# A decoder layer on one core: where the squares of x, the storing of weight parts and the V joins stand in a hand-written order

## The chip, the core and the metric

The kernel runs on one core of one Trainium2 chip. The metric is the device time of one execution in microseconds (us), as the median of the runs. The engines named below are TensorE (PE for its matmuls, PEld for its weight loads), VectorE (DVE), ScalarE (ACT), GpSimd (POOL, here mostly an issuer of transfers) and SyncE (SP, which issues most transfers).

## The reference

One layer of a decoder for 1024 positions of width 2048, all in float32. The input is normalised, and one projection makes the queries, keys, values and gates of two groups of eight heads: a stick-breaking group ("sb" below) and a differential group ("df", two softmax maps subtracted). Both outputs are gated, joined, projected and added to the residual; then a per-layer embedding is gated with a sigmoid of the normalised residual and added, and a last norm closes.

```python
hn = rmsnorm(h, norm_mix_g[i])
proj = hn @ w_in[i]
sb_q, sb_k, sb_v, sb_g, df_q, df_k, df_v, df_g = jnp.split(proj, split_at, axis=-1)
sb_out = stick_breaking_attention(sb_q, sb_k, sb_v)        # (1, 1024, 8, 128)
df_out = differential_attention(dq, dk, df_v, lam)         # rotary on a quarter of each q and k
df_out = rmsnorm(df_out, subln_g[i], SUBLN_EPS) * (1.0 - lambda_init)
mixed = jnp.concatenate([sb_out * jax.nn.silu(sb_g), df_out * jax.nn.silu(df_g)], axis=-1)
h = h + mixed @ w_out[i]
gate = jax.nn.sigmoid(rmsnorm(h, norm_ple_g[i]) @ w_ple_gate[i])
h = h + gate * (p[i] @ w_ple_proj[i])
return rmsnorm(h, norm_final_g)
```

## The kernel before

Every float32 product is made of three matmuls of split operands (high by high, high by low, low by high), so every weight tile is cast once to its high part (on ACT) and subtracted once for its low part (on DVE) before PE can use it. The 1024 rows are two halves of 512; the causal maps are made for half 1 first, then for half 0.

The stages, by time in the profile: up to about 630 us the V and gate columns of the projection; 630 to 1080 us the q and k products and the attention of half 1; 1080 to 1640 us the same for half 0; then the output projection (to about 1960 us) and the embedding's gate (to the end).

**The first stage** is an instance `gv` of the class `Seven`. It makes each pair of output blocks out of seven products instead of eight (a Strassen-like scheme with summed inputs S1 to S4 and summed weights T, L761), for 16 units of columns. One product is twelve matmuls of 512 columns, some 2.72 us, and is called a slot: `Seven.step` is run after each, casts the next weight tiles (`wpr`, L802 on ACT and L816 on DVE), does what is due and calls `chore(slot)`. In the first phase a unit has five slots (S2, A22, S1, S4, S3, where A22 and S4 are of the unit before), in the second phase, from slot 79 on, seven (A11, A22, S2, S4, A12, S1, S3). What follows a product is also fixed: for S3 the sum `u` on DVE (L1242 in the kernel before), after which the PSUM bank `pbc` can be written by the next unit.

**What hangs on the slots** besides the products, in `chore`:

- The sum of squares of x for the norm (`square`): 32 tiles `xs` of 128x512 are loaded by SP (L1057); three slots later ACT squares one (L1061 for the first of each half, L1063) and DVE adds it to `ssa` (L1064). `TICK["rows"]` is the slot of the first. The tiles have the tag "xt", four buffers that they share with the `xv` tiles of the sums S1 to S4 just ahead of them (stored to `xcomb_d` by POOL), with the chores' tiles and, later, with the V joins.
- `joint`: the sums over the partitions and the Newton steps of the square root, at fixed slots.
- The chores themselves: 32 weight tiles (of `w_out` and of the last pair of heads' `w_in`) that will be needed later as parts are loaded (`craw`, L1122), split into `chi` (ACT L1127) and `clo` (DVE L1128), and stored by SP (L1117, L1118).

**The attention** runs over pairs of heads, a df head and then an sb head, while PE makes the q and k products of the next (`acc`, L295 to L297). What stands beside them on DVE and ACT is placed in a queue of steps by ticks (`Side.add`, `side.later`; 32 ticks to a unit of products). The table `TICK` holds all ticks; a name with `mid_` or `end_` ahead replaces the plain one for the last pair of half 1 and of half 0 (`tk`). The steps that matter here, for a row block of a df head: scores `z` on PE (L381 to L388), row maximum on DVE (L435, `mx`), exponential on ACT (L443, `et`), the inverse of the sums and lambda on DVE (L448, L449), a scaling on ACT (L453), the difference of the two maps on DVE (L458, `et`), its transposes on PE (L493, `tp`), their split in two parts (L511 and L512 on ACT, L516 `lead` and L517 `awl` on DVE), and the product with V on PE (L535 to L540, `av`). `values` joins V for one head: it comes from DRAM as two planes of 16-bit halves (`vf`), is put together by two ACT copies (L474, `vw`), cast to its high part on ACT (L475) and subtracted on DVE (L478). In half 1 it is also stored for half 0.

For PE, DVE and ACT the program's order is the order written by hand (`tc.manual_schedule`); SP and POOL are ordered by the scheduler. In the middle seam ("turn"), where half 1 hands over to half 0, ACT and DVE also make the split x of half 0 (`xh` L1315, `xl` L1316).

Of the kernel before, what the change touches and what calls it, by code (L numbers as in the profile page):

```python
# [39 lines left out]
GLAT = {'S4': 4, 'S1': 4, 'S2': 4, 'S3': 3}  # L40
TICK = {
    "neg": 2, "cs": 27, "x0_at": (7, 7, 8, 7), "end_df_soft": (1, 1.5, 4.5, 5.5), "df_inv": 4, "mid_df_inv": 2.7,
    "end_df_inv": 4.5, "sumlag": 2, "gvx": ((22, 27), (80, 85)), "chore": (85, 0, 0), "rows": 19, "opx": (8, 12), "turn": 76, "lag":
    15, "gap": (4, 6), "parts": (1, 2), "vparts": (2, 3), "sums": (0, 2), "squared": (3, 4.5), "norm": (1, 4), "df_scores":
    (-20, -16, -13, -8, -4, 0, 4, 8), "df_turn": (19, 19), "df_v": -6, "df_norm": 44.5, "sb_scores": (-2, 5.5, 13.5, 22),
    "sb_turn": (32, 36), "sb_v": 19, "df_soft": (1, 1.5, 4, 5.5), "sb_stick": (1, 1, 3, 5.5), "taken": (28, 31), "sb_split":
    (1, 2), "kv": 9, "df_vg": (25, 42, 58, 59.5), "sb_vg": (4, 16, 24, 25.5), "q_turn": (-1.0, 5.5, 5, 6.5, 10, 12,
# [5 lines left out]
    70), "begun": (86.5, 91.5, 93.5, 94.5, 93.5), "mid_turn": 76, "mid_lag": 17, "mid_gap": (4, 7), "mid_df_scores": (-20,  # L53
    -16, -9, -8.5, -1, -0.5, 4, 8), "mid_df_turn": (19, 17), "mid_df_v": -6, "mid_df_norm": 44.5, "mid_sb_scores": (-3, 5,
    12.5, 21), "mid_sb_turn": (32, 36), "mid_sb_v": 18, "mid_taken": (28, 31), "mid_q_turn": (-1.5, 4.5, 4.5, 5.5, 9.5,
    11.5, 12.5), "mid_k_turn": (-1.5, 8, 8.5, 9, 13.5, 15, 16, 17.5), "end_turn": 76, "end_lag": 15, "end_gap": (4, 6),
    "end_df_scores": (-23, -16, -15, -8, -4, 0, 4, 8), "end_df_turn": (18.5, 19), "end_df_v": -6, "end_df_norm": 44.5,
    "end_sb_scores": (-2, 6, 13.5, 22), "end_sb_turn": (32, 36), "end_sb_v": 19, "end_taken": (28, 31), "end_q_turn": (-1.0,
    5, 5, 6.5, 10, 12, 13.5), "end_k_turn": (-4.5, 8, 8.5, 10, 13.5, 15, 16, 17.5),
}  # L60
# [4 lines left out]
def build(nc, tc, ap):  # L65
    with ExitStack() as ctx:
        _body(ctx, nc, tc, ap)


def _body(ctx, nc, tc, ap):  # L70
# [7 lines left out]
    V, G, A, T = nc.vector, nc.gpsimd, nc.scalar, nc.tensor  # L78
# [200 lines left out]
    side = Side()  # L279
# [67 lines left out]
    def attention(at, pz, half, hd, q, qz, K, KL, VV, sg, vg, rcol):  # L347
# [119 lines left out]
        def values():  # L467

            v = at.tile([P, 2, 4, P], F32R, name="v", tag="v")
            whole = ev.tile([P, 4, P], F32, name="vw", tag="xt", bufs=4)  # L470
            words = whole.bitcast(U16).rearrange("p a (b c) -> p a b c", c=2)
            planes = vg[0].bitcast(U16).rearrange("p (c a b) -> p c a b", c=2, a=4)
            for c in range(2):
                A.copy(words[:, :, :, c], planes[:, c])  # L474
            side.later(TICK["vparts"][0], lambda: A.copy(v[:, 0], whole))  # L475

            def low():
                V.tensor_tensor(v[:, 1], whole, v[:, 0].bitcast(F32), op=ALU.subtract)  # L478
                if half == 1:
                    G.dma_start(v_d[hd], v.rearrange("p a b c -> p (a b c)"))  # L480

            side.later(TICK["vparts"][1], low)
            VV.insert(0, v)

        def turn(pr, g):
# [147 lines left out]
    with tc.tile_pool(name="at", bufs=2) as at, tc.tile_pool(name="pz", bufs=2, space=PSUM) as pz:  # L633
# [420 lines left out]
        def square(kt, hf):  # L1054

            t = ev.tile([P, HALF], F32, name="xs", tag="xt", bufs=4)
            nc.sync.dma_start(t, xsrc(hf, kt))  # L1057

            def fn():
                if kt == 0:  # L1060
                    A.activation(ssa[hf], t, AF.Square)  # L1061
# [33 lines left out]
        chores = deque()  # L1095
# [5 lines left out]
        work, done = [], []  # L1101

        rows = deque((kt, hf) for kt in range(NK) for hf in (1, 0))
        fetched = deque()

        def chore(slot):
            q = slot - TICK["rows"]
            if q >= 0 and fetched and fetched[0][0] <= slot:
                fetched.popleft()[1]()
            if q >= 0 and rows and (q * 11) % 16 < 11:  # L1110
                fetched.append((slot + 3, square(*rows.popleft())))
            if slot in joint:
                joint.pop(slot)()
            if slot % 3 == 0 and done:
                (hi, lo), hi_d, lo_d = done.pop()
                if hi_d is not None:
                    nc.sync.dma_start(hi_d.bitcast(F32), hi.bitcast(F32))  # L1117
                nc.sync.dma_start(lo_d.bitcast(F32), lo.bitcast(F32))  # L1118
            if slot % 3 == 0 and chores and slot >= TICK["chore"][0] and not TICK["chore"][1] <= slot < TICK["chore"][2]:
                src, hi_d, lo_d = chores.popleft()  # L1120
                raw = ev.tile([P, HALF], F32, name="craw", tag="xt", bufs=4)
                nc.sync.dma_start(raw, src)  # L1122
                work.append((raw, hi_d, lo_d))
            elif slot % 3 == 2 and work:
                raw, hi_d, lo_d = work.pop()
                hi, lo = [ev.tile([P, HALF], F32R, name=nm, tag="xt", bufs=4) for nm in ("chi", "clo")]
                A.copy(hi, raw)  # L1127
                V.tensor_tensor(lo, raw, hi.bitcast(F32), op=ALU.subtract)  # L1128
                done.append(((hi, lo), hi_d, lo_d))
# [32 lines left out]
        def root(hf):  # L1162
            A.activation(ssa[hf], totals[hf], AF.Ln, bias=eps6[:, 0:1], scale=1.0 / NK)
            A.activation(ssa[hf], ssa[hf], AF.Exp, scale=-0.5)
            rstds[hf] = ssa[hf]

        def refined(hf, i):
            if i == 0:
                steps[hf] = ev.tile([P, HALF], F32, name="nt", tag="xt", bufs=4)
            t, ps, r = steps[hf], totals[hf], ssa[hf]  # L1170
            if i == 0:
                V.scalar_tensor_tensor(t, ps, EPS * NK, r, op0=ALU.add, op1=ALU.mult)
            elif i == 1:
                V.scalar_tensor_tensor(t, t, -0.5 / NK, r, op0=ALU.mult, op1=ALU.mult)
            else:
                V.scalar_tensor_tensor(r, t, 1.5, r, op0=ALU.add, op1=ALU.mult)

        joint = {67: partial(split_sum, 1), 68: partial(split_sum, 0), 70: lambda: (total(1), total(0)), 71: partial(root, 1), 73: partial(root, 0)}
        joint.update({72 + i: partial(refined, 1, i) for i in (0, 2)})
        joint[73] = lambda: (refined(1, 1), root(0))  # L1180
        joint.update({75 + i: partial(refined, 0, i) for i in range(3)})
        joint[79] = consts_late

        parts_of = {}

# [291 lines left out]
        for half in (1, 0):  # L1477
            X = X0 if half == 0 else X1

            for hd in ORDER:  # L1480
# [110 lines left out]
                q, k, qz, KL = qk[0], qk[1], qk.get("qz"), qk.get("kl")  # L1591
# [894 lines left out]
```

## Time and profile before

| | |
|---|---|
| median of 3 runs | 2323.59 us (2322.37 to 2324.1) |
| the profiled execution | 2324.44 us, of which 2322.6 us are the profile's span |
| granted TensorE clock, mean | 0.998 |
| PE matmuls | 2294.8 us busy, 99% of the span |
| DVE | 1816.6 us, 78% |
| ACT | 1341.1 us, 58% |
| POOL | 320.9 us, 14% |
| transfers | 565.05 MB, 243 GB/s on average |

A line of the timeline has the start in us, the duration, the engine, the line of the program, the operation and what it writes from what it reads; brackets at its end hold the idle time of that engine just before, and what ended it. A group of several instructions in one line has their count behind an x. A line of waits has the engine and the operation that waited, what for, and then the total, the number and the longest in us. A line of windows has the stretch and its length, then busy us of PE, PEld, DVE, ACT and POOL with their counts, the granted clock, the share of the DMA engines' time and GB/s. Because the matmuls' ends are modelled and overlap, a stall of PE is seen earlier in the weight load's record (PEld) than in the matmul's.

### The profile page before, as it was taken

The page shows a single profiled execution, that of the slowest core. Times are in us where ns is not written, and L with a number is a line of the kernel's source. Part 1 is how long each engine was busy: PE and PEld are TensorE (multiplying, and loading weights), DVE is VectorE, ACT ScalarE, POOL GpSimd, SP SyncE. Part 2 cuts the span into 40 slices and gives each one's busy share as a digit, 9 for nine tenths or more (in the row PEclk, how much of TensorE's full clock was granted, in tenths as well). Part 3 has the DMA queues.
Part 4 walks back from the last instruction along what each step waited for, and adds up shares of the span by engine and source line. Part 5 has one row for each costly group of instructions (what it writes and reads, how often), then busy time and mean ns, then how long its engine had stood idle before and what let it go on. Part 6 is the DMA issues. An engine that isn't in the chain of part 4 may idle for free.

```text
span 2322.6 us, 32653 instructions
## 1 busy us (share of the span) xinstructions
PE 2294.8 (99%) x10961; PEld 1916.6 (83%) x10961; DVE 1816.6 (78%) x3155; ACT 1341.1 (58%) x2420; POOL 320.9 (14%) x498
## 2 busy tenths in 40 slices
PE   9999999999999999999999999999999999999998
PEld 7877888888788888887888888888888888888887
DVE  6578887777668888878778777778787988687787
ACT  6424354444357777778877777777733435542555
POOL 2121111111211111101011001110121121111000
PEclk9999999999999999999999999999999999999999
DMA  8687678877798888899676677777999789998975
GB/s 260 214 295 252 202 247 239 247 211 199 208 271 276 244 256 240 250 282 315 199 218 186 182 208 209 204 199 239 269 213 244 248 246 282 313 357 269 298 239 199
DMA packets 290200, 565.05 MB, mean 243 GB/s; under 512 B 62688, under 2 KB 73184, under 8 KB 290032
## 3 DMA queue, kind: packets, MB, share of 16 engines
q1 hardware_dynamic: 219216, 383.34, 53.0%
q0 software_dynamic: 58864, 158.10, 24.7%
q10 hardware_dynamic: 11952, 21.53, 2.6%
q8 instruction: 86, 1.41, 0.3%
q14 instruction: 82, 0.67, 0.1%
HBM read 359.16 MB, written 203.69 MB: 242 GB/s over the span
## 4 chain that ended last, share of the span: by engine, by line
PE 61%; issue 18%; DVE 8%; DMA 4%; ACT 4%; POOL 3%; SPq 0%; POOLq 0%; DVEq 0%; ACTq 0%
PE acc L297 8%; PE acc L295 8%; PE acc L296 8%; PE pbc L707 7%; PE pa L707 5%; PE pc L707 4%; PE tp L493 2%; POOL vg_d L915 2%; PE pb L707 2%; PE av L540 1%; PE av L539 1%; PE av L538 1%; PE pc L1904 1%; PE pc L1903 1%; PE pc L1902 1%
## 5 line engine op out<-in xcount | busy, mean ns | idle before, releaser
L802 ACT CAST wpr<-T 128x512 fp32r<-128x512 f32 x208 | 127.3, 620 | 423.1 <-DVE T L761 362.8
L295 PE MATMUL acc<-xh,whi 128*128 128x512 f32 x768 | 310.2, 404 | 0.0
L297 PE MATMUL acc<-xh,wlo 128*128 128x512 f32 x768 | 300.6, 391 | 0.0
L296 PE MATMUL acc<-xl,whi 128*128 128x512 f32 x768 | 300.5, 391 | 0.0
L297 PEld LDWEIGHTS acc<-xh,wlo 128*128 128x128 f32 x768 | 144.2, 188 | 31.8
L295 PEld LDWEIGHTS acc<-xh,whi 128*128 128x128 f32 x768 | 145.1, 189 | 25.1
L296 PEld LDWEIGHTS acc<-xl,whi 128*128 128x128 f32 x768 | 144.8, 189 | 24.4
L802 ACT CAST wpr<-wraw 128x512 fp32r<-128x512 f32 x128 | 78.6, 617 | 124.5 <-DMA wraw<-tw_d 37.3
L816 DVE TENSOR_TENSOR wpr<-T,wpr 128x512 fp32r<-128x512 f32 x208 | 142.4, 685 | 8.4 <-ACT wpr L802 6.7
L200 ACT CAST whi<-wraw 128x1024 fp32r<-128x1024 f32 x128 | 134.3, 1049 | 13.4 <-DMA wraw<-w_in 7.4
L443 ACT ACTIVATE et<-z,mx 128x512 f32<-128x512 f32 (+7 forms) x128 | 94.8, 741 | 56.9 <-DVE mx L435 56.5
L707 PE MATMUL pbc<-cA,wpr 128*128 128x512 f32 x480 | 117.5, 394 | 5.0 <-DVE u L1242 4.6
L517 DVE TENSOR_TENSOR awl<-tp,awh 128x256 fp32r<-128x256 f32 (+1 forms) x160 | 92.6, 579 | 33.5 <-ACT awh L512 32.9
L707 PE MATMUL pc<-cS,wpr 128*128 128x512 f32 x480 | 115.3, 389 | 0.0
L707 PE MATMUL pbc<-cS,wpr 128*128 128x512 f32 x480 | 115.3, 389 | 0.0
L707 PEld LDWEIGHTS pbc<-cA,wpr 128*128 128x128 f32 x480 | 90.3, 189 | 26.6 <-DVE u L1242 7.5
L435 DVE CUSTOM_DVE_ANT_0 z<-z,wide 128x512 f32<-128x512 f32 (+7 forms) x128 | 97.5, 763 | 18.5 <-PE z L388 16.0
L707 PE MATMUL pbc<-cS2h,wpr 128*128 128x512 f32 x320 | 105.7, 391 | 0.0
L707 PEld LDWEIGHTS pc<-cS,wpr 128*128 128x128 f32 x480 | 90.1, 188 | 18.7
L707 PEld LDWEIGHTS pbc<-cS,wpr 128*128 128x128 f32 x480 | 90.1, 188 | 18.7
L707 PE MATMUL pc<-cS4h,wpr 128*128 128x512 f32 x320 | 105.0, 389 | 0.0
L915 POOL DMA_DIRECT2D vg_d<-hc x96 | 62.6, 652 | 302.1 <-DVE hc L1140 167.1
(556 smaller groups left out, 6460.4 us busy)
## 6 DMA issues: line engine op xcount, KB each, us to landing
wraw<-w_in SPq DMA_DIRECT2D x128, 512.0 KB, 4.7
wraw<-w_vg SPq DMA_DIRECT2D x143, 256.0 KB, 3.7
wlo_d<-wlo POOLq DMA_DIRECT2D x56, 512.0 KB, 6.5
vg_d<-hc POOLq DMA_DIRECT2D x96, 256.0 KB, 4.3
wlo<-wlo_d SPq DMA_DIRECT2D x48, 512.0 KB, 3.8
wraw<-w_gate SPq DMA_DIRECT2D x92, 256.0 KB, 5.5
h_d<-hc POOLq DMA_DIRECT2D x56, 256.0 KB, 5.4
wraw<-w_out SPq DMA_DIRECT2D x56, 256.0 KB, 4.9
```

The source lines that it names most:

```text
L200: side.later(1, lambda: A.copy(hi[:, o], raw[:, o]))
L295: T.matmul(acc[c], hi[:, k2, kh, c, :], xh, start=first, stop=False)
L296: T.matmul(acc[c], hi[:, k2, kh, c, :], xl, start=False, stop=False)
L297: T.matmul(acc[c], lo[k2][:, kh, c, :], xh, start=False, stop=last)
L435: V.tensor_tensor_reduce(z[:, vw], z[:, vw], add, -DF_SCALE, 3.0e38, ALU.add, ALU.min, mx)
L443: A.activation(et[:, vw], z[:, vw], AF.Exp, bias=mx[:, 0:1], scale=-1.0, accum_out=l[:, c:c + 1])
L493: T.transpose(tp[:, j, b * P:(b + 1) * P], ws[2 * pr + b][:, (g0 + j) * P:(g0 + j + 1) * P], ident)
L517: V.tensor_tensor(wl[:, o, :], tp[:, o, :], wh[:, o, :].bitcast(F32), op=ALU.subtract)
L707: T.matmul(o, a[:, w], x, start=start and k + i == 0, stop=k == 3 and i == 2, skip_group_check=True)
L802: A.copy(t[:, 0], src)
L816: V.tensor_tensor(t[:, 1], src, t[:, 0].bitcast(F32), op=ALU.subtract)
L915: G.dma_start(vg_d[hf, blk, u], o, **(dict(accum_op=ALU.add) if ph else {}))
```

## The change

It moves work and changes no arithmetic. Four things:

1. The squares start at slot 25 instead of 19, and come in 4 slots out of 5 instead of 11 out of 16. `joint` comes four slots later throughout, `consts_late` nine.
2. The chores start at slot 86, and have fixed places in a unit of seven slots: a store and the next load in slots 1 and 4 counted from slot 86 (chore's `at_`), a cast and subtraction in slots 0 and 3. Before they came in every third slot whatever the unit. The last four steps no longer fit, and are put at ticks 4, 7, 12 and 15 of the first attention unit.
3. V of a df head is joined 9.5 ticks earlier (`df_v` and `end_df_v` from -6 to -15.5), and its load is asked for 5 ticks earlier (`df_vg`).
4. In the last df head of half 1, V is joined 6.5 ticks later (`mid_df_v` from -6 to 0.5), with its two parts one tick sooner after it (`mid_vparts`).

```diff
-    ... "chore": (85, 0, 0), "rows": 19, ... "df_v": -6, ... "df_vg": (25, 42, 58, 59.5), ...
+    ... "chore": 86, "rows": 25, ... "df_v": -15.5, ... "df_vg": (20, 42, 58, 59.5), ...
-    ... "mid_df_v": -6, ... "end_df_v": -6, ...
+    ... "mid_vparts": (1, 2), "mid_df_v": 0.5, ... "end_df_v": -15.5, ...
...
-            side.later(TICK["vparts"][0], lambda: A.copy(v[:, 0], whole))
+            side.later(tk("vparts")[0], lambda: A.copy(v[:, 0], whole))
...
-            if q >= 0 and rows and (q * 11) % 16 < 11:
+            if q >= 0 and rows and q % 5 < 4:
                 fetched.append((slot + 3, square(*rows.popleft())))
...
-            if slot % 3 == 0 and done:
+            at_ = (slot - TICK["chore"]) % 7 if slot >= TICK["chore"] else None
+            if at_ in (1, 4) and done:
                 (hi, lo), hi_d, lo_d = done.pop()
...
-            if slot % 3 == 0 and chores and slot >= TICK["chore"][0] and not TICK["chore"][1] <= slot < TICK["chore"][2]:
+            if at_ in (1, 4) and chores:
                 src, hi_d, lo_d = chores.popleft()
...
-            elif slot % 3 == 2 and work:
+            elif at_ in (0, 3) and work:
                 raw, hi_d, lo_d = work.pop()
...
-        joint = {67: partial(split_sum, 1), 68: partial(split_sum, 0), 70: lambda: (total(1), total(0)), 71: partial(root, 1), 73: partial(root, 0)}
+        joint = {71: partial(split_sum, 1), 72: partial(split_sum, 0), 74: lambda: (total(1), total(0)), 75: partial(root, 1)}
...
-        joint[79] = consts_late
+        joint[88] = consts_late
...
+        side.add([(t, partial(chore, TICK["chore"] + 7 * 15 + k)) for t, k in ((4, 3), (7, 4), (12, 7), (15, 8))])
```

What this does to the order on the engines is shown at three places. Lines of the changed kernel are one higher from L1114 on, two higher from about L1278 on.

ScalarE in the first stage, where the first squares (L1061) stand among the weight casts (L802, L800), before:

```order
L802 CAST wpr<-T_1466 128x512
L802 CAST wpr<-T_1463 128x512
L1061 ACTIVATE ssa<-xs 128x512
L802 CAST wpr<-T_1492 128x512
L800 ACTIVATE wpr<-b_848 128x512
L1061 ACTIVATE ssa<-xs 128x512
L802 CAST wpr<-T_1550 128x512
L1063 ACTIVATE xs<-xs 128x512
```

And in the changed kernel, from the same weight cast on:

```order
L802 CAST wpr<-T_1462 128x512
L802 CAST wpr<-T_1459 128x512
L802 CAST wpr<-T_1485 128x512
L800 ACTIVATE wpr<-b_848 128x512
L802 CAST wpr<-T_1540 128x512
L802 CAST wpr<-T_1567 128x512
```

Neither of the two squares is left among these casts; they follow six places further down.

VectorE at the end of a second-phase unit, one in three, before (`clo` is the chore's subtraction, `u` at L1242 the sum after S3):

```order
L816 TENSOR_TENSOR wpr<-T_3680,wpr 128x512
L816 TENSOR_TENSOR wpr<-wraw,wpr 128x512
L1128 TENSOR_TENSOR clo<-craw,chi 128x512
L1242 TENSOR_TENSOR u_3731<-pbc,s_3568 128x512
L1261 TENSOR_TENSOR hc<-pc,u_3731 128x512
L761 TENSOR_TENSOR T_3751<-wraw 128x512
```

The same place in the changed kernel:

```order
L816 TENSOR_TENSOR wpr<-wraw,wpr 128x512
L1243 TENSOR_TENSOR u_3719<-pbc,s_3560 128x512
L1262 TENSOR_TENSOR hc<-pc,u_3719 128x512
L761 TENSOR_TENSOR T_3739<-wraw 128x512
L761 TENSOR_TENSOR T_3742<-b_848,T_3739 128x512
L816 TENSOR_TENSOR wpr<-wraw,wpr 128x512
L1129 TENSOR_TENSOR clo<-craw,chi 128x512
L816 TENSOR_TENSOR wpr<-T_3742,wpr 128x512
```

The chore's subtraction no longer stands ahead of `u`, but between two low parts of weights (`wpr`, L816) behind it.

VectorE in a df head of half 0, before, where the V join's subtraction is L478:

```order
L435 ISA z,mx<-z,wide 128x896
L435 ISA mx 128x1
L448 RECIPROCAL l<-l 128x2
L449 TENSOR_TENSOR l<-l,lam 128x1
L478 TENSOR_TENSOR v<-vw,v 128x512
L554 TENSOR_REDUCE sm<-av 128x128
L556 TENSOR_TENSOR sg<-sm,sg 128x256
L435 ISA z,mx<-z,wide 128x768
L435 ISA mx 128x1
L458 SCALAR_TENSOR_TENSOR et<-et,l 128x896
```

In the changed kernel it stands a row block earlier, ahead of that block's inverse (L448, L449) and of the `awl` that follows it (L517):

```order
L1540 TENSOR_TENSOR q<-qk,q 128x512
L1536 TENSOR_TENSOR qk<-acc_11099,ssa 128x512
L478 TENSOR_TENSOR v<-vw,v 128x512
L448 RECIPROCAL l<-l 128x2
L449 TENSOR_TENSOR l<-l,lam 128x1
L435 ISA z,mx<-z,wide 128x896
L435 ISA mx 128x1
L517 TENSOR_TENSOR awl<-tp,awh 128x512
```

At its old place L554 now follows L449 directly. On ScalarE its two copies and its cast moved from behind the second L512 and the L453 of the block to the place just ahead of the L443 of the block before.

More of the change, by code (lines that the diff above doesn't have):

```diff
@@ L42 @@
     "neg": 2, "cs": 27, "x0_at": (7, 7, 8, 7), "end_df_soft": (1, 1.5, 4.5, 5.5), "df_inv": 4, "mid_df_inv": 2.7,
-    "end_df_inv": 4.5, "sumlag": 2, "gvx": ((22, 27), (80, 85)), "chore": (85, 0, 0), "rows": 19, "opx": (8, 12), "turn": 76, "lag":
+    "end_df_inv": 4.5, "sumlag": 2, "gvx": ((22, 27), (80, 85)), "chore": 86, "rows": 25, "opx": (8, 12), "turn": 76, "lag":
     15, "gap": (4, 6), "parts": (1, 2), "vparts": (2, 3), "sums": (0, 2), "squared": (3, 4.5), "norm": (1, 4), "df_scores":
-    (-20, -16, -13, -8, -4, 0, 4, 8), "df_turn": (19, 19), "df_v": -6, "df_norm": 44.5, "sb_scores": (-2, 5.5, 13.5, 22),
+    (-20, -16, -13, -8, -4, 0, 4, 8), "df_turn": (19, 19), "df_v": -15.5, "df_norm": 44.5, "sb_scores": (-2, 5.5, 13.5, 22),
     "sb_turn": (32, 36), "sb_v": 19, "df_soft": (1, 1.5, 4, 5.5), "sb_stick": (1, 1, 3, 5.5), "taken": (28, 31), "sb_split":
-    (1, 2), "kv": 9, "df_vg": (25, 42, 58, 59.5), "sb_vg": (4, 16, 24, 25.5), "q_turn": (-1.0, 5.5, 5, 6.5, 10, 12,
+    (1, 2), "kv": 9, "df_vg": (20, 42, 58, 59.5), "sb_vg": (4, 16, 24, 25.5), "q_turn": (-1.0, 5.5, 5, 6.5, 10, 12,
     13.5), "k_turn": (-4.5, 8, 8.5, 10, 13.5, 15, 16, 17.5), "x0": ((3, 5, 13, 12), (6, 7, 14, 15), (5, 6, 14, 16), (5, 5,
@@ L53 @@
     70), "begun": (86.5, 91.5, 93.5, 94.5, 93.5), "mid_turn": 76, "mid_lag": 17, "mid_gap": (4, 7), "mid_df_scores": (-20,
-    -16, -9, -8.5, -1, -0.5, 4, 8), "mid_df_turn": (19, 17), "mid_df_v": -6, "mid_df_norm": 44.5, "mid_sb_scores": (-3, 5,
+    -16, -9, -8.5, -1, -0.5, 4, 8), "mid_df_turn": (19, 17), "mid_vparts": (1, 2), "mid_df_v": 0.5, "mid_df_norm": 44.5, "mid_sb_scores": (-3, 5,
     12.5, 21), "mid_sb_turn": (32, 36), "mid_sb_v": 18, "mid_taken": (28, 31), "mid_q_turn": (-1.5, 4.5, 4.5, 5.5, 9.5,
     11.5, 12.5), "mid_k_turn": (-1.5, 8, 8.5, 9, 13.5, 15, 16, 17.5), "end_turn": 76, "end_lag": 15, "end_gap": (4, 6),
-    "end_df_scores": (-23, -16, -15, -8, -4, 0, 4, 8), "end_df_turn": (18.5, 19), "end_df_v": -6, "end_df_norm": 44.5,
+    "end_df_scores": (-23, -16, -15, -8, -4, 0, 4, 8), "end_df_turn": (18.5, 19), "end_df_v": -15.5, "end_df_norm": 44.5,
     "end_sb_scores": (-2, 6, 13.5, 22), "end_sb_turn": (32, 36), "end_sb_v": 19, "end_taken": (28, 31), "end_q_turn": (-1.0,
@@ L480, in low @@
                     G.dma_start(v_d[hd], v.rearrange("p a b c -> p (a b c)"))
-            side.later(TICK["vparts"][1], low)
+            side.later(tk("vparts")[1], low)
             VV.insert(0, v)
@@ L1176, in refined @@
                 V.scalar_tensor_tensor(r, t, 1.5, r, op0=ALU.add, op1=ALU.mult)
-        joint = {67: partial(split_sum, 1), 68: partial(split_sum, 0), 70: lambda: (total(1), total(0)), 71: partial(root, 1), 73: partial(root, 0)}
-        joint.update({72 + i: partial(refined, 1, i) for i in (0, 2)})
-        joint[73] = lambda: (refined(1, 1), root(0))
-        joint.update({75 + i: partial(refined, 0, i) for i in range(3)})
-        joint[79] = consts_late
+        joint = {71: partial(split_sum, 1), 72: partial(split_sum, 0), 74: lambda: (total(1), total(0)), 75: partial(root, 1)}
+        joint.update({76 + i: partial(refined, 1, i) for i in (0, 2)})
+        joint[77] = lambda: (refined(1, 1), root(0))
+        joint.update({79 + i: partial(refined, 0, i) for i in range(3)})
+        joint[88] = consts_late
         parts_of = {}
```

## Prediction

> **What bounds the kernel now.** I read the page's busy times first, then what TensorE's weight loads waited for over the whole span, then busy time by stretch, then the waits of each stretch that the change touches.
>
> ```profile
> span 2322.6 us, 32653 instructions
> PE 2294.8 (99%) x10961; PEld 1916.6 (83%) x10961; DVE 1816.6 (78%) x3155; ACT 1341.1 (58%) x2420; POOL 320.9 (14%) x498
> PEld tp L493 <- DVE et L458: 7.5, 15, 1.4
> PEld pbc L707 <- DVE u L1242: 7.5, 6, 3.9
> PEld av L535 <- DVE lead L516: 5.0, 8, 0.8
> ```
>
> TensorE (PE) is busy 2294.8 of 2322.6 us, so all that a reordering can win is in its 27.8 idle us, plus matmuls that ran slowly. PE keeps its instructions and their order, but for the sums of squares (ssps), which come four slots later. A weight load's wait is nearer to the lost time than the matmul's own, because a matmul's record covers the first part of a stall; 0.04 us of each is the normal gap. The two largest groups, u (L1242) and et (L458), stand behind operations that this change moves; lead (L516) does not.
>
> ```profile
> 160.00:200.00 40.00, 35.54 (x146) 27.94 (x146) 31.72 (x51) 16.10 (x29) 4.88 (x9) 0.96 0.86 284
> 200.00:240.00 40.00, 40.00 (x178) 33.14 (x177) 34.38 (x55) 15.66 (x28) 4.88 (x9) 1.00 0.72 223
> 440.00:480.00 40.00, 39.52 (x173) 31.98 (x173) 28.34 (x45) 16.46 (x31) 5.71 (x8) 1.00 0.78 228
> ```
>
> The columns after the window's length are PE, PEld, DVE, ACT and POOL busy with counts, then the granted clock, the DMA share and GB/s. The window from 160 to 200 us does 146 matmuls where the next does 178: 32 x 40/178 = 7.2 us of product time are lost there, at a clock of 0.96. It is the largest hole in the kernel.
>
> **Squares six slots later (first stall).** What holds PE there:
>
> ```profile
> SPq L1057 <- DMA xcomb_d<-xv: 3.4, 1, 3.4
> xs<-xT SPq DMA_DIRECT2D x32, 256.0 KB, 3.5
> 162.85 0.63 ACT L1061 ACTIVATE ssa<-xs 128x512 f32<-128x512 f32 x1 [5.59 <-DMA xs<-xT]
> 167.63 0.63 ACT L1061 ACTIVATE ssa<-xs 128x512 f32<-128x512 f32 x1 [3.11 <-DMA xs<-xT]
> 173.27 0.50 PE L707 MATMUL pb<-cS2h,wpr 128*128 128x512 f32 x1 [0.71 <-ACT wpr L802]
> 180.08 4.27 PE L707 MATMUL pbc<-cA,wpr 128*128 128x512 f32 x12 [3.51 <-DVE u L1242]
> 189.97 2.88 PE L707 MATMUL pb<-cS,wpr 128*128 128x512 f32 x12
> PEld pbc L707 <- DVE u L1242: 4.6, 2, 3.9
> ```
>
> Read it downwards. SP holds the loads of xs back for stores of xv, which use the same four buffers. The first two squares (L1061) already have their place in ACT's stream, so ACT stands 5.59 and 3.11 us with the weight casts (L802) queued behind them, and DVE, whose squares' sums (L1064) stand ahead of u, is late after ACT. PE then waits for wpr at 173.27 and for u at 180.08. Three products lie between 180.08 and 189.97, 9.89 us for 3 x 12 x 40/178 = 8.1: another 1.8 us goes in matmuls that ran slowly after the stall. Of the two waits for u (4.6), the one that isn't the 3.9 is 0.7 us near 161, behind DVE's own work; it stays. 7.2 - 0.7 = **-6.5 us**. It goes because the loads come six slots on: ACT reached slot 22 at 162.85 - 5.59 = 157.26, so slot 28 is at 157.26 + 6 x 2.72 = 173.6, and its load is asked for 3 slots (8.2 us) ahead, past the xv stores that SP waited for; the landing takes 3.5 in the median. No load is added; the 32 are only moved on SP past xv's stores and some weight loads, and come a little closer together.
>
> On the 1.8 us: the granted clock of the window is 0.96, of its neighbour 1.00. [...]
>
> What it costs: squares run at 4 of 5 slots, not 11 of 16, 16% more DVE and ACT work in slots 28 to 65, and the joint root is 4 slots later.
>
> ```profile
> 320.00:360.00 40.00, 40.00 (x178) 33.13 (x177) 34.08 (x58) 20.68 (x37) 5.35 (x8) 1.00 0.76 234
> 640.00:680.00 40.00, 40.00 (x186) 33.47 (x185) 23.59 (x42) 20.46 (x33) 5.52 (x10) 1.00 0.86 256
> ```
>
> DVE adds one L1064 (0.69) per square: 14.7 slots in 40 us x (0.8 - 0.6875) x 0.69 = 1.1 us on 34.38 (the window 200 to 240), 89% full, still under 40. The joint moves three operations of some 0.6 us into a stretch at 34.08. Between zero (slack holds) and 1.8 us (all three on the path) I take **+0.5**, nearer to zero since nothing stalls PE at 320 to 360 now.
>
> **Weight parts at fixed slots (phase 1).** Window 440 to 480 lost (178 - 173) x 0.225 = 1.1 us. Its cause, and in the last two rows what such waits sum to from 400 to 630 us:
>
> ```profile
> 469.92 0.62 ACT L802 CAST wpr<-wraw 128x512 fp32r<-128x512 f32 x1 [3.48 <-DMA wraw<-w_vg]
> 471.09 0.69 DVE L1128 TENSOR_TENSOR clo<-craw,chi 128x512 fp32r<-128x512 f32 x1 [4.63 <-ACT chi L1127]
> 471.70 0.69 DVE L1242 TENSOR_TENSOR u<-pbc,s 128x512 f32<-128x512 f32 x1
> PEld pbc L707 <- DVE u L1242: 2.9, 4, 0.9
> PEld pbc L707 <- DVE wpr L816: 1.6, 4, 0.4
> ```
>
> In every third unit a chore's cast stands in the last slot: chi waits on ACT behind a late wraw, clo waits for chi, and u (the start of A22's product) waits for clo. With casts at slots 0 and 3 of a unit alone, clo never stands ahead of u. 2.9 + 1.6 less 8 x 0.04 = **-4.2 us**. What may come instead: the thin margin of a cast in slot 0, which all units will now have.
>
> ```profile
> 454.80 0.69 DVE L816 TENSOR_TENSOR wpr<-T,wpr 128x512 fp32r<-128x512 f32 x1
> 455.71 0.41 PEld L707 LDWEIGHTS pbc<-cS2h,wpr 128*128 128x128 f32 x2
> ```
>
> This unit already has casts at 0 and 3 and does not stall: L816 ends 455.49 and the weight load that needs it comes 0.22 us later. The chores that slip into the first attention unit meet DVE at 23.59 and ACT at 20.46 of 40 us; cover enough, with an upper bound of one clo, 0.69. I take **+0.3** for both.
>
> **V's join, half 0.**
>
> ```profile
> 1189.39 1.12 ACT L443 ACTIVATE et<-z,mx 128x1024 f32<-128x1024 f32 x1 [2.04 <-DVE mx L435]
> 1192.74 0.69 DVE L517 TENSOR_TENSOR awl<-tp,awh 128x512 fp32r<-128x512 f32 x1 [0.50 <-ACT awh L512]
> 1193.74 0.19 PEld L540 LDWEIGHTS av<-awl,v 128*128 128x128 f32 x1
> 1201.02 0.69 DVE L478 TENSOR_TENSOR v<-vw,v 128x512 fp32r<-128x512 f32 x1 [1.85 <-ACT v L475]
> 1203.43 1.15 DVE L458 SCALAR_TENSOR_TENSOR et<-et,l 128x896 f32<-128x896 f32 x1
> PEld tp L493 <- DVE et L458: 4.3, 7, 0.8
> PEld tp L493 <- DVE et L458: 0.8, 1, 0.8
> ```
>
> DVE stands 1.85 us at L478, for ACT's L475 of the V join, with L458 behind it; PE's transposes wait for L458 once per pair (the last two rows: 4.3 us in 1085 to 1600, 0.8 at the end seam). Without L478 there, L458 would end some 1.85 us earlier, well ahead. (4.3 + 0.8) - 8 x 0.04 = **-4.8 us**. Where V goes, ACT idles 2.04 us ahead of L443: two L474 copies and L475 fill it and no more. But L478 (0.69) now stands ahead of L448 and L449 on DVE, which release L453, L512 and L517 in turn. L517 ends 1193.43, L540's weights are wanted at 1193.74: a 0.4 to 0.5 us delay overshoots the 0.31 us by 0.1 to 0.2. Six pairs: **+0.9 us** (0 to 2).
>
> **V's join, half 1 and the middle.**
>
> ```profile
> PEld tp L493 <- DVE et L458: 0.9, 6, 0.2
> PEld tp L493 <- DVE et L458: 1.4, 1, 1.4
> PEld z L381 <- ACT et L443: 1.3, 1, 1.3
> 1070.42 1.42 ACT L474 COPY vw<-vf 128x512 uint16<-128x512 uint16 x2
> 1071.67 0.75 ACT L1315 ACTIVATE xh<-xl,gvec 128x512 fp32r<-128x512 f32 x1
> 1078.09 0.47 ACT L443 ACTIVATE et<-z,mx 128x256 f32<-128x256 f32 x1 [0.92 <-DVE mx L435]
> ```
>
> The first row is half 1 up to its middle (636 to 1063 us), the next two the middle (1063 to 1082). In half 1 the same move takes away six small waits: 0.9 - 6 x 0.04 = **-0.7**. In the middle head the turn's xh (L1315) waits behind L474; behind the turn instead, L1315 and everything after come 1.24 us earlier and the 1.4 us wait goes. But V's copies then stand ahead of the last L443, whose z PE wants 1.33 us earlier: that wait stays and may grow by 0.5. Net **-0.9** (0 to -2.4).
>
> **The sum.** -6.5 + 0.5 - 4.2 + 0.3 - 4.8 + 0.9 - 0.7 - 0.9 = -15.4. A shift of this size also makes waits of its own where transfers and DVE stood just in time; the awl overshoot shows how close they are. I take +1 for those unnamed (0 to 3): -14.4. The profiled execution took 2324.44 us, 0.85 above the median of 2323.59; from the median, 2323.6 - 14.4 = 2309.2, rounded to 2309.5 because the largest terms are upper sizes. Ends: all costs at zero, -17.1 and the whole middle, -18.6, 2305; all costs at their upper bounds (1.8 + 0.7 + 2 + 0.9 + 3 against 17.1), -8.7, 2315.
>
> **Rivals.**
> 1. The cast at slot 0 stalls S2 in each unit. For it: 0.22 us of margin and 16 units; against: the units with that pattern do not stall. At 0.2 us in 14 units +2.8: 2312.
> 2. The first stall only moves. The denser squares make DVE (89% by the sum above) late with u, or ACT waits for xs again because its landing exceeds the 3 slots of lead. For it: the DMA share of 0.86 in 160 to 200, with 16% more squares per us to come. Against: 3 slots are 8.2 us against a median landing of 3.5, and the window 200 to 240 has all its 178 matmuls with squares in it. It gives back 6.5: 2316.
> 3. Slower: the fixed places make one slot-6 kind of stall in every unit. SP issues the chore's stores in order, and the weight loads stand behind them:
>
> ```profile
> SPq L1118 <- DVE clo L1128: 39.6, 14, 5.9
> ACT wpr L802 <- DMA wraw<-w_vg: 29.4, 10, 3.5
> ```
>
> SP stood 39.6 us at L1118 between 400 and 630, and ACT 29.4 us for wraw between 340 and 640. If each of 15 units paid the 4.2/3 = 1.4 us that one in three pays now, that is +21 instead of -4.2: 2323.6 - 10.2 (the rest of the sum) + 21 = 2334. From 1.0 us per unit on the change is slower than before by over 0.2%. Against: u no longer stands behind clo, so only a wraw later than now can do it.
> 4. No effect in half 0: V's copies land on ACT late all the same, because vf or DVE's mx is late, and the wait moves to awl. Then 4.8 is lost: 2314.
>
> **Chances.** The forecast case with its costs between the bounds 0.60; rival 1 0.12; rival 2 0.11; rival 4 0.09; rival 3 0.03; two of the rivals 1, 2 and 4 together, 2317 to 2321, 0.05, mostly within 0.2%. 0.2% is 4.6 us, about what a measurement of this kernel can tell from no change, so faster means under 2318.9: 0.93; same 0.04; slower, rival 3, 0.03. The range 2304.5 to 2316.5 takes in the forecast, and rivals 1, 2 and 4.
>
> **What would show it.** The 160 to 200 window with 175 or more matmuls at a clock of 1.00, ACT's waits for xs under 1 us; no wait of pbc for u in 400 to 630; transposes' waits for L458 near zero in half 0, and awl (L540) instead with six small ones; z (L381) at 1.3 to 1.9 in the middle; lead's 5.0 unchanged. Wrong it is if a window between 200 and 360 holds under 176 matmuls, or if wpr waits appear in each unit of phase 1.

## The result

The changed kernel took 2307.89 us (median of 4 runs, 2305.51 to 2309.46) against 2323.85 us for the kernel before (4 runs, 2322.37 to 2324.82): a ratio of 0.9931, 95% interval 0.9914 to 0.9948, or 16 us less. Run again later, five times (e11 below), it took 2305.09 against 2323.26 us: 0.9927 (0.9914 to 0.9939). The times are medians, the ratios are of the means. One execution of e12 took 3230.03 us at a granted clock of 0.66, and is left out of that run's median and ratio. The forecast was 2309.5.

The page of the changed kernel, span and busy times, and then the larger of the weight loads' waits over its span (engine, waiter, releaser; total us, times, longest):

```profile
span 2303.6 us, 32654 instructions
PE 2287.5 (99%) x10961; PEld 1915.9 (83%) x10961; DVE 1818.4 (79%) x3155; ACT 1339.2 (58%) x2420; POOL 321.3 (14%) x498
```

```profile
PEld av L535 <- DVE lead L516: 3.4, 8, 0.7
PEld av L540 <- DVE awl L517: 2.2, 3, 1.4
PEld z L381 <- ACT et L443: 1.9, 1, 1.9
...
PEld pbc L707 <- DVE u L1243: 1.1, 2, 0.7
PEld pbc L707 <- ACT part L1203: 1.0, 1, 1.0
...
PEld tp L493 <- DVE et L458: 0.2, 1, 0.2
```

The two groups that led before are gone: tp for et has fallen from 7.5 to 0.2 us, pbc for u from 7.5 to 1.1. The waits for lead fell as well, from 5.0 to 3.4, which was not forecast. The window with the hole, and the one with the chore's stall, are full:

```profile
160.00:200.00 40.00, 40.00 (x178) 33.12 (x177) 36.03 (x58) 18.40 (x32) 4.88 (x9) 1.00 0.89 302
440.00:480.00 40.00, 40.00 (x179) 33.10 (x178) 28.56 (x45) 16.14 (x29) 5.72 (x8) 1.00 0.81 242
```

To see where the 19.0 us between the two profiled spans come from, I read the start of the same TensorE instruction in both timelines at six places: an A22 product ahead of the hole (133.76 us before, 132.00 after), an A22 product behind it, 25 products on (209.01, 200.53), the first and the sixth wait for lead in half 1 (716.82 and 993.25; 705.94 and 979.90), the first L535 of the second head of half 0 (1096.10, 1081.90) and one at its end (1635.80, 1617.18). The differences are the stages of this table; the runs are those of the next section.

| stage, us | before | after | squares alone (e1) | chores alone (e2) | V alone (e3) |
|---|---|---|---|---|---|
| start to the first mark | 133.76 | 132.00 | 132.16 | 132.35 | 132.18 |
| the hole | 75.25 | 68.53 | 68.53 | 75.73 | 76.03 |
| rest of the first stage, to lead | 507.81 | 505.41 | 508.45 | 504.84 | 506.81 |
| half 1, five pairs | 276.43 | 273.96 | 276.42 | 276.70 | 273.69 |
| middle | 102.85 | 102.00 | 102.76 | 104.16 | 102.67 |
| half 0 | 539.70 | 535.28 | 540.48 | 540.11 | 535.21 |
| to the end | 686.80 | 686.42 | 685.70 | 684.81 | 686.01 |

Of the 19.0 us, 17.2 lie behind the first mark, where the change is. The 1.8 ahead of it are not the change's: every later run, of either first stage, reached the first mark at 131.9 to 133.3 us. The execution that was profiled before was late there (last section).

The runs of the next section are one execution each, but for e8, e11 and e12, so I compare their stages and not their times. A stage that a run leaves as it was varies too: the hole with the old squares takes 75.2 to 76.0 us, the rest of the first stage with the old chores and the old joint 506.6 (e4) to 507.8, the stage to the end 684.8 to 689.4.

One sign that the prediction had named as showing it wrong did come: a window between 200 and 360 us with under 176 matmuls. In the changed kernel 320 to 360 holds 175 (176 in e11), where the kernel before had 178:

```profile
320.00:360.00 40.00, 40.00 (x175) 32.47 (x175) 34.38 (x59) 19.08 (x36) 6.23 (x9) 1.00 0.73 212
```

The sign was set tighter than the prediction's own sum: three matmuls are some 0.7 us, and the sum had +0.5 for the denser squares and the later joint, which is what they cost (below).

### The profile page after: what moved, and what is told of

The parts are those of the page before. It is cut to its first block, busy times and chain, and to the rows that moved or that the text cites. A ratio compares the mean times of both kernels' runs of the same rounds, so it can differ in the third digit from the quotient of the medians.

```text
span 2303.6 us, 32654 instructions
## 1 busy us (share of the span) xinstructions
PE 2287.5 (99%) x10961; PEld 1915.9 (83%) x10961; DVE 1818.4 (79%) x3155; ACT 1339.2 (58%) x2420; POOL 321.3 (14%) x498
## 4 chain that ended last, share of the span: by engine, by line
PE 61%; issue 7%; DVE 2%; POOL 2%; DMA 1%; ACT 1%; POOLq 0%; DVEq 0%; SPq 0%; ACTq 0%
PE acc L295 10%; PE acc L297 10%; PE acc L296 10%; PE tp L493 3%; PE pb L1904 2%; PE pb L1905 2%; PE pb L1906 2%; PE z L388 1%; PE av L540 1%; PE pbc L707 1%; PE z L387 1%; PE pa L707 1%; PE pc L1904 1%; PE pc L1906 1%; PE pc L1905 1%
## 5 line engine op out<-in xcount | busy, mean ns | idle before, releaser
L802 ACT CAST wpr<-T 128x512 fp32r<-128x512 f32 x208 | 127.6, 620 | 429.0 <-DVE T L761 354.2
L802 ACT CAST wpr<-wraw 128x512 fp32r<-128x512 f32 x128 | 78.7, 617 | 127.6 <-DMA wraw<-w_vg 35.1
L816 DVE TENSOR_TENSOR wpr<-T,wpr 128x512 fp32r<-128x512 f32 x208 | 142.3, 684 | 6.0 <-ACT wpr L802 5.4
L517 DVE TENSOR_TENSOR awl<-tp,awh 128x256 fp32r<-128x256 f32 (+1 forms) x160 | 92.7, 579 | 34.4 <-ACT awh L512 33.9
L443 ACT ACTIVATE et<-z,mx 128x512 f32<-128x512 f32 (+7 forms) x128 | 95.0, 742 | 38.0 <-DVE mx L435 37.8
```

The costliest lines, as they stand in the source:

```text
L443: A.activation(et[:, vw], z[:, vw], AF.Exp, bias=mx[:, 0:1], scale=-1.0, accum_out=l[:, c:c + 1])
L517: V.tensor_tensor(wl[:, o, :], tp[:, o, :], wh[:, o, :].bitcast(F32), op=ALU.subtract)
L802: A.copy(t[:, 0], src)
L816: V.tensor_tensor(t[:, 1], src, t[:, 0].bitcast(F32), op=ALU.subtract)
```

## The experiments

**Parts one at a time.** Theory: each stall was one engine standing, in order, behind one late operand, so that the parts of the change act each in its own stage and add. Rival: they hang together through the transfers.

*e1, the squares.* The kernel before with this:

```diff
-"chore": (85, 0, 0), "rows": 19
+"chore": (85, 0, 0), "rows": 25
-(q * 11) % 16 < 11
+q % 5 < 4
-joint = {67: ..., 68: ..., 70: ..., 71: ..., 73: ...}; ...; joint[79] = consts_late
+joint = {71: ..., 72: ..., 74: ..., 75: ...}; ...; joint[88] = consts_late
```

> The kernel before with the first part of the change alone: squares from slot 25 at 4 of 5 slots, the joint root 4 slots later, the late constants 9 later; chores and V joins as before. Theory of parts that add (each stall is one engine standing in order behind one late operand): the 160 to 200 us window goes from 146 to 178 matmuls, worth 6.7 us, the later joint costs 0.6 us near 330 us, the chores' waits near 414, 472, 530 and 588 us stay at 3.5 us together and the V waits stay. Sum -6.1, about 2318. Rival: the parts hang together (the freed transfers or the shifted slots also move the chores): the chores' waits change by more than 1 us, and the time is outside 2315 to 2321 by the stage's marks.

It took 2316.28 us (the kernel before 2322.96 beside it), and the hole is 68.53 us as in the full change. In the rest of the stage it is 0.64 slower than before, 0.51 of it near 330 us, by the starts of the products.

*e2, the chores.* The kernel before with the new places of the chores alone.

> The kernel before with the chores' fixed places alone (slots 1 and 4 store and load, 0 and 3 cast; the last four steps in the first attention unit). Theory: the nine waits from 414 to 592 us vanish, -3.5 us, one wait near 613 to 624 us for the ACT copy of part grows from 0.5 to 1.0 us, so -2.9; the hole at 160 to 200 stays at 146 matmuls. Rival: the waits vanish only because the squares and the joint shifted; then part of them is still there, -1 or less.

2320.47 us. No wait at all is left between 340 and 610 us, the wait for part is 0.99, and the rest of the first stage is 507.81 - 504.84 = 2.97 us shorter. The hole stays.

*e3, V.* The kernel before with this:

```diff
-"df_v": -6, "end_df_v": -6, "df_vg": (25, ...
+"df_v": -15.5, "end_df_v": -15.5, "df_vg": (20, ...
```

> The kernel before with V joined 9.5 ticks earlier in df heads of both halves and the load 5 ticks earlier; the middle head as before. Theory: half 1 is 2.6 us shorter although the transposes' waits there are worth 0.7 only, since VectorE's 1.25 us stand at L478 is carried to lead (L516) in the sb head 30 us later; half 0 4.4 us shorter with no new wait for awl. Sum -7. Rival: half 1's surplus of 1.9 us came from the moved chores or from the shift against the transfers; then half 1 gains 0.7 here, and the sum is -5.

2314.49 us; half 1 is 2.74 us shorter and half 0 4.49. So the surplus of half 1 is V's own. With the middle's 0.85, which is the whole change's own number since that part was not run alone, the parts add to 6.72 - 0.64 + 2.97 + 2.74 + 4.49 + 0.85 = 17.1, as the whole did behind the first mark (17.2, with 0.4 in the last stage). So the parts add, as far as the variation of the stages lets one say.

**What of the V join cost the time.** *e4* leaves the ACT copies, the cast and the load where they were, and moves one VectorE instruction:

```diff
-side.later(TICK["vparts"][1], low)
+side.later(TICK["vparts"][1] if hd < H else 6, low)
```

> The kernel before with only VectorE's subtraction of the V join (L478) of the df heads moved, from 3 to 6 ticks behind the join's start; the ACT copies and the cast stay where they were, and so does the load. Theory: what cost time was VectorE standing at L478 for ACT's cast, with L458 behind it; so the transposes' waits for L458 go as in the changed kernel, half 1 gains 1.5 to 2.6 us and half 0 3.5 to 4.4 us, sum -5 to -7. Rival: ACT's own 2 us of V work in that place is what delays the maximum, the exponential and L458; then the waits stay within a third of what they were, and the sum is 0 to -2.

2314.19 us: half 1 took 273.73 us (-2.70) and half 0 534.47 (-5.23), at least as good as the earlier join. Here is the stand that was taken away, in half 1 of the kernel before, and behind it what the weight loads waited for in half 1 (640 to 1040 us) in e1, where V is as before, and in e4:

```profile
740.23 0.69 DVE L478 TENSOR_TENSOR v<-vw,v 128x512 fp32r<-128x512 f32 x1 [1.25 <-ACT v L475]
741.18 0.61 DVE L458 SCALAR_TENSOR_TENSOR et<-et,l 128x384 f32<-128x384 f32 x1
```

```profile
PEld av L535 <- DVE lead L516: 4.2, 6, 0.8
PEld tp L493 <- DVE et L458: 0.9, 6, 0.2
```

```profile
PEld av L535 <- DVE lead L516: 2.4, 6, 0.4
```

VectorE stood 1.25 us at L478 for ACT's cast, with L458 behind it. That made the transposes late by 0.15 us a pair. The rest of the delay stayed. At L448, just ahead of this place, the kernel before is 3.05 us behind e4 (738.61 against 735.56), as at the mark of 716.82. From the row maximum at 743.45 us on it is 3.5 to 3.6 us behind, on both engines. Here are ScalarE's next exponential and the lead of the next head, first in the kernel before, then in e4:

```profile
743.97 0.47 ACT L443 ACTIVATE et<-z,mx 128x256 f32<-128x256 f32 x1 [1.21 <-DVE mx L435]
771.80 0.27 DVE L516 TENSOR_TENSOR lead<-tp,lead 128x128 fp32r<-128x128 f32 x1
```

```profile
740.39 0.47 ACT L443 ACTIVATE et<-z,mx 128x256 f32<-128x256 f32 x1 [0.83 <-DVE mx L435]
768.19 0.27 DVE L516 TENSOR_TENSOR lead<-tp,lead 128x128 fp32r<-128x128 f32 x1
```

VectorE did stand idle in between, 1.58 us before L1518 alone, but it was waiting there for ScalarE. ScalarE was late too, since it had waited for VectorE's maximum. So lead, 30 us later, let TensorE wait 0.4 us longer than in e4. ACT's 2 us of V work at that place were harmless: without the stand at L478 both losses are gone.

**How much shift the squares needed.** *e5*, *e6*, *e9* and *e10* start them at slot 20 or 22, at the new rate (4 of 5 slots) or the old one (11 of 16); the rest is the changed kernel.

> The changed kernel with the squares starting at slot 20 instead of 25 (rate and joint as changed). [...] Rival: the squares simply do not fit at that place of the stream, whatever the transfers; then the hole is as in the kernel before, 146 matmuls, 7 us lost, about 2315. Third: one slot is enough, under 1 us lost.

> The changed kernel with the squares starting at slot 22. Theory of the late transfer: first and second square are due near 165.4 and 168.1 us, when xs has landed as in the kernel before (162.9 and 167.6), so no wait of u or wpr of more than 0.3 us is left in 160 to 200: three of the six slots buy all 6.7 us, and the rest of the shift is margin. Rival: the gain grows evenly with the shift; then half of it, 3.3 us, is still lost here, and the window does about 162 matmuls.

> The changed kernel with the squares starting at slot 20 and at the old rate of 11 in 16. With the denser rate that start lost 6.4 us in the hole where I had expected 2.5 to 4. Theory: the late transfers set the loss and the denser squares added the rest, since they put more VectorE sums ahead of u; then with the old rate 3 to 4.5 us are lost, between the phase marks 71.5 to 73 us instead of 74.9, and the clock stays at 0.98 or more. Rival: the rate does not matter, and a shift of one slot buys next to nothing; then 6 to 6.5 us are lost again and the clock is 0.96.

> The changed kernel with the squares starting at slot 22 and at the old rate of 11 in 16. With the denser rate 1.3 us were left of the hole (u late by 1.16 and 0.51). Theory of the rate: both waits fall to 0.3 us or less, 68.5 to 68.8 us between the marks. Rival, the transfers: xs still lands 1.4 us behind its place, and 0.8 us or more are lost.

| first load in slot | rate | second square in slot | the hole, us | lost against 68.53 | clock, 160 to 200 |
|---|---|---|---|---|---|
| 19 (before) | 11/16 | 24 | 75.25 | 6.7 | 0.96 |
| 20 (e5) | 4/5 | 24 | 74.93 | 6.4 | 0.96 |
| 20 (e9) | 11/16 | 25 | 70.17 | 1.6 | 1.00 |
| 22 (e6) | 4/5 | 26 | 69.87 | 1.3 | 1.00 |
| 22 (e10) | 11/16 | 27 | 68.78 | 0.2 | 1.00 |
| 25 (after) | 4/5 | 29 | 68.53 | 0 | 1.00 |

A square stands three slots behind its load, which gives the third column. Only e10 came out as its theory had it. e5 lost 6.4 us at a clock of 0.96, where I had estimated 2.5 to 4 at 1.00, e9 1.6 and not 3 to 4.5, and e6 still 1.3 where I expected next to nothing. ScalarE's wait for the first two squares' xs is alike in e5 and e9 (140 to 205 us), but VectorE's wait for ScalarE's squares behind them is not (two rows of e5, then two of e9):

```profile
ACT ssa L1061 <- DMA xs<-xT: 6.3, 2, 3.5
DVE ssa L1064 <- ACT xs L1063: 8.3, 6, 4.7
```

```profile
ACT ssa L1061 <- DMA xs<-xT: 6.9, 2, 4.1
DVE ssa L1064 <- ACT xs L1063: 4.6, 5, 2.0
```

TensorE's waits in 165 to 215 us differ accordingly (three rows of e5, then one of e9):

```profile
PEld pbc L707 <- DVE u L1243: 3.2, 2, 2.8
PEld pb L707 <- DVE wpr L816: 1.9, 1, 1.9
PEld pb L707 <- ACT wpr L802: 0.4, 1, 0.4
```

```profile
PEld pbc L707 <- DVE u L1243: 2.0, 2, 1.3
```

In e5 the clock falls too, which takes another 1.7 us (one product of twelve matmuls takes 4.45 us from start to start instead of 2.72). The rate does two things at once: it sets how much work a slot holds, and it sets in which slot the second and third squares stand. In e5 these stand in slots 24 and 25, as in the kernel before, and in e9 in 25 and 26, behind one more weight cast. The six losses follow the second square's slot without exception. So the gain is neither even in the shift of the first square nor all in its first slot. Whether the denser work costs anything beyond that slot, these runs do not separate; with the transfers long landed, at slot 25, this place of the stream shows no loss.

**The prediction's slower rival.** *e7* puts the casts in slots 3 and 6, so that clo stands directly ahead of u in 14 units (of the four last steps in the attention, the cast moves with them):

```diff
-elif at_ in (0, 3) and work:
+elif at_ in (3, 6) and work:
```

> The changed kernel with the chores' casts in slots 3 and 6 of each unit instead of 0 and 3 (stores and loads stay at 1 and 4), so that clo stands directly ahead of u in 14 of the units. This is rival 3 of the prediction made on purpose. By the theory that the place ahead of u is what costs: in the kernel before three to five units with this order lost 0.8 to 1.7 us each, so 14 units lose 11 to 20 us, and the time is 2319 to 2328. Rival: it is the late wraw of single units that costs, and clo is only where it shows; then two to five units lose 1 to 1.5 us, and the time is 2310 to 2314.

2313.55 us, and the rest of the first stage took 512.08 us, 6.7 more than the changed kernel. The weight loads' waits in 340 to 610 us, where the changed kernel has none:

```profile
PEld pbc L707 <- DVE u L1243: 5.0, 7, 1.1
PEld pbc L707 <- DVE wpr L816: 3.2, 9, 0.4
PEld pbc L707 <- ACT wpr L802: 0.4, 2, 0.2
```

The time lies in the range of the rival, the mechanism between the two: the place ahead of u costs, but by the low parts' waits in 9 units of the 14, and 0.5 us a unit over all 14, not 1.4. That a late wraw picks these units, as the rival had it, was not traced unit by unit. Half 0 took 537.94 us, 2.7 more than in the changed kernel, for a reason of its own (last section). Even with this place in every unit the change stays faster than the kernel before.

**Toward a better version.** *e8* adds three edits to the changed kernel, *e12* only the first two; *e11* is the changed kernel once more, beside e12.

```diff
-joint = {71: ..., 72: ..., 74: ..., 75: ...}
+joint = {68: ..., 69: ..., 71: ..., 72: ...}
-"df_v": -15.5, "end_df_v": -15.5, "df_vg": (20, ...    side.later(tk("vparts")[1], low)
+"df_v": -6, "end_df_v": -6, "df_vg": (25, ...          side.later(tk("vparts")[1] if sb or seam == "mid_" else 6, low)
-"mid_df_v": 0.5          (e8 alone)
+"mid_df_v": 2
```

> The changed kernel with three edits: the joint root 3 slots earlier (one slot later than in the kernel before), V of the df heads joined where the kernel before had it but with VectorE's subtraction 6 ticks behind the copies, and V of the middle head 1.5 ticks later, behind the last row block's exponentials. Theory: the wait at 330 us goes (-0.6), half 0 gains another 0.7 as in the run with the subtraction alone, the wait for z in the middle falls from 1.9 to 0.5 (-1.4): -2.7 against the changed kernel, 2305 against 2323.5. Rival: the edits in the middle only move the wait to the transposes of the last block, and the later chain of the seam; then -1 to -1.5, about 2306.5.

> The changed kernel once more, beside the next one on the same chip, for the comparison of the two and for its spread: 2306 to 2310, ratio 0.993.

> The changed kernel with the two edits that held: the joint root 3 slots earlier, and V of the df heads joined where the kernel before had it, with VectorE's subtraction 6 ticks behind the copies; the middle head as in the changed kernel. By the stage marks of the earlier run: -0.5 in the first stage, -0.7 in half 0, so 1.2 us less than the changed kernel on the same chip, ratio 0.9925. Rival: the runs' spread of 2 us hides it; then the medians differ by less than 0.5 either way and only the marks show it.

e8 took 2305.47 us, ratio 0.9928 (0.9914 to 0.9941); e12 2304.75 (four executions), 0.9921 (0.9905 to 0.9936); e11 2305.09, 0.9927 (0.9914 to 0.9939), a little under what I expected of it. The runs don't tell the three apart. The stages do: in e12 the rest of the first stage is 504.85 us against 505.42 of e11 (the wait at 330 us has gone), half 0 534.00 against 535.17, and the middle 103.29 against 101.96, which takes 1.3 of these 1.7 us back for a reason of its own (last section). The third edit brought 0.3 us in the middle (102.95 in e8 against e12's 103.29) where I expected 1.4. The wait only moved, as its rival had it, though to another place: the wait for z fell from 1.9 to 0.5, but V then was not ready for its product. In e8, 1060 to 1070 us:

```profile
PEld av L535 <- ACT v L475: 0.6, 1, 0.6
PEld av L535 <- DVE v L478: 0.5, 1, 0.5
PEld z L381 <- ACT et L443: 0.5, 1, 0.5
```

## Why the prediction was right, step by step

*Squares, -6.5.* Measured -6.72, by the mechanism that was named: ScalarE has no wait for xs left there, the window is full, and its clock is 1.00. That the 1.8 us of slow matmuls in this term would go with the stall was an estimate; no run shows what lowers the clock, only that with the squares moved the hole went from 75.25 to 68.53 us (e1 and the changed kernel) and the window's clock from 0.96 to 1.00 (changed kernel). *Their cost, +0.5.* Measured 0.6: in the changed kernel the joint's three Newton steps for half 0 stand in the full stretch, and u comes late behind the four splits (L688) that follow:

```profile
318.15 0.68 DVE L1177 SCALAR_TENSOR_TENSOR ssa<-nt,ssa 128x512 f32<-128x512 f32 x1
...
326.34 2.50 DVE L688 TENSOR_TENSOR cS4l<-cS4l,cS4h 128x512 fp32r<-128x512 f32 x4
328.76 0.68 DVE L1243 TENSOR_TENSOR u<-pbc,s 128x512 f32<-128x512 f32 x1
```

With the joint three slots earlier (e8, e12) the wait is gone. The denser squares cost nothing at this place, but rival 2 was nearer than I gave it: at slot 20 the new rate, which puts the second square a slot earlier, made 4.8 us of difference.

*Chores, -4.2 and +0.3.* The nine waits went, and with them 3.5 us, not 4.2: their records come to 4.56 us, and the starts of the products show 3.45, so that each was worth 0.12 us less than its record, where I took off 0.04. What came instead was not the thin margin of rival 1, of which no trace shows anything, but half a microsecond at the end of the stage, where the wait for ACT's copies of part grew from 0.5 to 1.0. Net -3.0 (e2) for a forecast of -3.9. And the loss itself is not steady: with the same old chores the starts of the products show 3.5 us in the execution before, 3.6 in e1, but 2.4 in e3 and 2.3 in e4. So this part is worth some 2 to 3 us, and the -4.2 was read off one of the costlier executions.

*Half 0, -4.8 and +0.9.* Measured -4.42, -3.9 forecast. The awl that I feared has no new wait in the table of waits, but the rows show it at the edge: L517 ends at 1179.11, and L540's weights go in at 1179.16, 0.44 us behind the first L538, where before it was 0.34.

```profile
1175.71 0.68 DVE L478 TENSOR_TENSOR v<-vw,v 128x512 fp32r<-128x512 f32 x1
...
1178.42 0.69 DVE L517 TENSOR_TENSOR awl<-tp,awh 128x512 fp32r<-128x512 f32 x1 [0.68 <-ACT awh L512]
```

```profile
1178.72 0.19 PEld L538 LDWEIGHTS av<-awh,v 128*128 128x128 f32 x1
...
1179.16 0.19 PEld L540 LDWEIGHTS av<-awl,v 128*128 128x128 f32 x1
```

Against e4, which leaves L448 free of L478, e3 loses 0.09 us at this place in each of six pairs and 0.2 more at the end seam, 0.74 together. The gross gain is then e4's 5.2 us (4.8 forecast) and the cost 0.7 (0.9 forecast): both were right in kind and near in size.

*Half 1, -0.7.* Measured -2.47 (e3 -2.74): the term that was furthest off. The step that failed was "lead (L516) does not": lead stands behind no moved operation within its head, but VectorE and ScalarE, each in its order, were still 0.5 us late from L478 in the head before. I had priced the wait that L478 caused, not the lateness that it left. The sign "lead's 5.0 unchanged" failed with it (3.4).

*Middle, -0.9.* Measured -0.85, with z's wait at 1.9, inside the 1.3 to 1.9 that was given. *Unnamed waits, +1.* Up to the last mark there were none over 0.2 us apart from those above. The forecast sum was -14.4, the stages gave -17.2, and the medians -16.0 and -18.2. Half 1 makes 1.8 of the difference, the unnamed 1.0 and half 0 0.5; that the chores gave 0.9 less than forecast hides a part of it. So the time came nearer than its terms: that much was luck.

## What to carry to other kernels

An engine that works in order and stands for a late operand can cost twice: at the wait that shows next, and in lateness that goes on (here 0.15 us a pair at the transposes, and 0.4 at lead 30 us later). Idle time on it is no slack when it comes from waiting for an engine that is late as well (the 1.58 us before L1518); so look for a second wait a full stage later. Here the cure was to move the instruction that waits, not the work that it waits for: one VectorE subtraction placed six ticks behind the copies instead of three was worth at least as much as a whole join placed earlier. And when several loads are late, ask for each instruction that takes one where it stands, not only for the first. Last, a stall's worth should be read from more than one execution.

## What the runs showed of the hardware

*The clock fell without one long stall.* In e5 no wait reached the 3.9 us of the kernel before: 1.9 and 2.8 us stood 5 us apart, and the 160 to 200 us window still came to a clock of 0.96, with the product after the second wait at 4.45 us instead of 2.72; waits of 1.3 and 0.7 us (e9) left it at 1.00. In e7 the clock fell to 0.66 late in half 0, behind waits of 1.17 and 1.37 us. In e1 it stayed at 1.00 behind nearly the same two, at the same instructions (e7's weight loads and window, then e1's):

```profile
1589.61 0.19 PEld L538 LDWEIGHTS av<-awh,v 128*128 128x128 f32 x1 [1.17 <-ACT awh L512]
1591.27 0.26 PEld L540 LDWEIGHTS av<-awl,v 128*128 128x128 f32 x1 [1.37 <-DVE awl L517]
1590.00:1595.00 5.00, 3.84 (x14) 3.35 (x14) 4.02 (x7) 4.64 (x11) 0.00 (x0) 0.66 0.71 229
```

```profile
1593.07 0.19 PEld L538 LDWEIGHTS av<-awh,v 128*128 128x128 f32 x1 [1.09 <-ACT awh L512]
1594.74 0.19 PEld L540 LDWEIGHTS av<-awl,v 128*128 128x128 f32 x1 [1.37 <-DVE awl L517]
1590.00:1600.00 10.00, 8.17 (x43) 6.59 (x42) 8.08 (x13) 9.26 (x16) 0.53 (x1) 1.00 0.86 295
```

So e1 against e7 shows that the length of the waits does not settle it. What else does, these runs do not show. In e7 the fall took 1.7 us (5 us at 0.66); with the wait for awh, which is 0.2 in the changed kernel, that is its slower half 0.

The profiled execution before also shows a lower clock in its first microseconds (before, then after):

```profile
5.00:10.00 5.00, 3.54 (x9) 2.21 (x10) 3.08 (x5) 3.17 (x7) 0.00 (x0) 0.75 0.96 336
```

```profile
5.00:10.00 5.00, 4.95 (x15) 2.87 (x15) 4.13 (x8) 4.13 (x8) 0.00 (x0) 1.00 1.01 354
```

ScalarE waited up to 1.75 us for a first x tile, against 0.68 in the changed kernel, and TensorE idled 1.5 us of these five. It was 1.1 us late at the fourth of its products' matmuls (7.69 against 6.57 us), and 1.8 by 12 us, which stayed so to the first mark. The code up to there is the same. (The 1.00 of the second row does not cover all of it: up to 6.6 us its matmuls, too, come 0.43 us apart, later 0.23.) That such starts are a part of the 4 us by which runs of one kernel differ is likely, but not shown, since only one execution of a run has a profile.

*A VectorE subtraction was longer beside a GpSimd operation.* In five of the fourteen profiles (e2, e4, e5, e8, e12) one VectorE subtraction of the k turn (L1575 in the changed kernel) took 2.79 us instead of 0.69. It met the one large elementwise operation on GpSimd (L1299). First VectorE and GpSimd in e12, then both in e11:

```profile
1034.85 3.50 DVE L1575 TENSOR_TENSOR kl<-qk,k 64x512 fp32r<-64x512 f32 x2
```

```profile
1035.15 2.64 POOL L1299 TENSOR_TENSOR cs<-cs,ssa 128x1024 f32<-128x1024 f32 x1 [4.63 <-DMA cs<-rope]
```

```profile
1035.69 1.39 DVE L1575 TENSOR_TENSOR kl<-qk,k 64x512 fp32r<-64x512 f32 x2
```

```profile
1036.67 2.68 POOL L1299 TENSOR_TENSOR cs<-cs,ssa 128x1024 f32<-128x1024 f32 x1 [5.07 <-DMA cs<-rope]
```

Where GpSimd had begun ahead of the second subtraction, that one ended 0.56 us after GpSimd's operation in e12 (0.55 in e5); where the subtractions were ahead, the two took their usual 1.39 us (e11) and 1.40 (changed kernel). L517 took its usual 0.69 us at 1037.57 in the changed kernel, within GpSimd's 1036.19 to 1038.98, so not every VectorE operation is longer there; which are, and why, these runs do not show. In e12 the wait for lead in the middle was 1.6 us, in the changed kernel 0.6. That it was this and not the placing of L478 that cost e12 its gain in the middle rests on these rows, since e2 (its middle took 104.16 us, against 102.85 before) and e5 have it without that edit; no run moves the GpSimd operation.
